# Expert layer: each kind of load on a queue of its own, in the order of the text, and a third weight tile asked for ahead

## The chip, the cores and the metric

The kernel runs on one core of one Trainium2 chip. The metric is device time in microseconds (us) of one execution, and a version is judged by the median of several runs. TensorE (PE in the profile) multiplies, VectorE (DVE) and ScalarE (ACT) do elementwise work, GpSimd (POOL) does a little elementwise work and the gathers, and SyncE (SP) only issues loads and stores. SP, ACT and POOL can each issue DMAs; each of them takes its instructions in order, so an instruction that waits holds up all that stand behind it on its engine.

## The reference, cut to what matters

The program is two transformer blocks, one behind the other. The change lies in the expert layer ("peer") of the first: 16384 single-neuron experts, of which each token picks 128 (8 heads with 16 each).

```python
def peer(xn, wq, keys, u, v):
    ...
    v1, i1 = lax.top_k(s1, PEER_TOPK)
    v2, i2 = lax.top_k(s2, PEER_TOPK)
    cand = (v1[..., :, None] + v2[..., None, :]).reshape(...)
    sc, ci = lax.top_k(cand, PEER_TOPK)
    e = i1[ci // PEER_TOPK] * PEER_NKEYS + i2[ci % PEER_TOPK]
    g = jax.nn.softmax(sc, axis=-1)
    hid = jnp.einsum('thkd,td->thk', u[e], xb)
    a = jax.nn.gelu(hid, approximate=False) * g
    return jnp.einsum('thk,thkd->td', a, v[e])
```

## The kernel before, in words

For 384 of the 512 tokens the kernel does not gather. It computes the hidden value of every expert and every token, sets the weights of the experts that were not picked to zero, and multiplies everything with all of v. The experts are cut into 128 blocks of 128 ("an expert" below is such a block, and a pair is two of them, even and odd). For the other 128 tokens it gathers the picked rows of u and v (`Rows`) and works on them with DVE.

The layer has three stretches.

- **Building** (`hidden`, 61 pairs). For each pair, two tiles of u (512 KB each, `raw`) come in on SP. ACT makes the high part `whi` of a tile, DVE the low part `wlo`, PE does 48 matmuls, ACT applies gelu, and the result goes to DRAM (`Gd`). Beside it runs a side stream, paced by estimated costs (`T16`, `T256`, `TLK`, `BUILD`, `ROW`, summed into `SHARE` and `UPACE`): first four blocks of top-k on DVE (`topk_block`), then 96 builds (`build`) of the choice weights (DVE `hot`, ACT `hot` and `ab`, PE `aps`), which go to DRAM in pieces (`Ad`), and all along the gathers of u and their dot products (`row`, `rhid`).
- **Changeover**. The last 16 pieces of `Ad` are stored, the last three pairs of `hidden` are done, and the first choice weights are read back.
- **Multiplying** (loop over `order`, 124 experts, then the last 4 together). Each expert takes a tile of v (`raw`, 512 KB), its hidden values (`gt`, one load of 384 KB for a pair, three buffers) and its choice weights (`at`, one load of 768 KB for four experts, two buffers). DVE multiplies them in place (`gt<-gt,at`, called G below), ACT and DVE split the product into `ah` and `al`, and PE does 24 matmuls. One row step (`ro`) on DVE goes with each expert, with a gather of v on POOL four steps ahead.

The order of instructions on each engine is set by a scheduler that starts from the order of the text and moves work by its own estimates, unless `keep_in_program_order` pins it. Before, all loads of `raw`, `gt` and `at` in the multiplying stretch stood on SP, in an order that the scheduler had made. `raw` has two buffers, `whi` and `wlo` three, `ah` and `al` five, a gathered row four.

Of the kernel before, what the change touches and what calls it, by code (L numbers as in the profile page):

```python
# [22 lines left out]
NM = 16  # L23
# [55 lines left out]
def setup(tc, es, A):  # L79
    g = Ctx()  # L80
    nc = tc.nc
    g.tc, g.nc, g.A = tc, nc, A
    g.const = es.enter_context(tc.tile_pool(name="const", bufs=1))
    g.res = es.enter_context(tc.tile_pool(name="res", bufs=1))
    g.wp = es.enter_context(tc.tile_pool(name="wp", bufs=3))
    g.np_ = es.enter_context(tc.tile_pool(name="np", bufs=2))
    c = g.const

    def cin(name, shape, now=True):
        t = c.tile(shape, F32, name="c_" + name)  # L90
        if now:
            nc.sync.dma_start(t, A[name])
        return t

    g.cin = cin
    g.vec = cin("vecs", [P, NVEC])
    g.ident = cin("ident", [P, P], False)
    g.ones = c.tile([P, P], F32, name="ones")
    nc.gpsimd.memset(g.ones, 1.0)
    g.eps = c.tile([P, 1], F32, name="eps")  # L100
    nc.gpsimd.memset(g.eps, EPS)
    g.zero = c.tile([P, 1], F32, name="zero")
    nc.gpsimd.memset(g.zero, 0.0)
    g.pre = {}
    g.queue = []
    g.h = [None] * KT
    h_tiles(g)
    return g


def h_tiles(g):
    for k in range(KT):
        g.h[k] = g.res.tile([P, T], F32, tag=f"h{k}", name=f"h{k}")
# [7 lines left out]
def wsrc(g, name, idx):  # L121
    a = g.A[name]
    for i in idx:
        a = a[i]
    return a


def wload(g, src, pool, hl):

    nc = g.nc  # L130
    _, a, b = src.shape
    raw = g.wp.tile([P, a, b], F32, tag="raw", name="raw", bufs=2)
    nc.sync.dma_start(raw, src)
    hi = pool.tile([P, a, b], F32R, tag="whi", name="whi", bufs=hl)
    nc.scalar.activation(hi, raw, AF.Copy)  # L135
    lo = pool.tile([P, a, b], F32R, tag="wlo", name="wlo", bufs=hl)
    nc.vector.tensor_tensor(lo, raw, r32(hi), op=ALU.subtract)  # L137
    return hi, lo


def wpre(g, name, *idx):

    key = (name, idx)
    if key not in g.pre:
        g.pre[key] = wload(g, wsrc(g, name, idx), g.wp, 3)


def wget(g, name, *idx):

    key = (name, *idx)  # L150
    wpre(g, *key)
    if key in g.queue[:1]:
        g.queue.pop(0)
        for k in g.queue[:2]:
            wpre(g, *k)
    return g.pre.pop((name, idx))


# [755 lines left out]

NK = 128
TOPK = 16
LAST = 4
N1 = 122
PARTS = 4
# [10 lines left out]

UH = 120

T16, T256, TLK, BUILD, ROW = 1.65, 2.3, 1.6, 1.5, 1.36
TOPKS = 16 * T16 + 3 + 8 * T256 + 8 * TLK + 2
BUILDS = NCK * (0.8 + CH // 4 * BUILD)
UPACE = UH * ROW / (3 * TOPKS + BUILDS)
# [3 lines left out]
class Rows:  # L940
# [29 lines left out]
    def choose(self, lists):  # L970
# [4 lines left out]
        else:  # L975
            t = self.p.tile([P, 3, NJ], F32, name="rl")
            n = 8 // RG
            nc.scalar.activation(t[0:GT].rearrange("p i (a b) -> p i a b", b=TOPK), lists[0:GT, :, 0:n], AF.Copy)
            for r in range(1, RG):
                nc.scalar.dma_start(t[r * GT:(r + 1) * GT].rearrange("p i (a b) -> p i a b", b=TOPK), lists[0:GT, :, r * n:(r + 1) * n])  # L980
            l = [t[:, i] for i in range(3)]
# [54 lines left out]
def peer_block(g, ni, tail):  # L1036

    tc, nc, A = g.tc, g.nc, g.A
    with ExitStack() as es:
        dr = es.enter_context(tc.tile_pool(name="p_dram", bufs=1, space=DRAM))  # L1040
        Gd = [dr.tile([P, 2, ND], F32, name=f"Gd{i}") for i in range(NK // 2)]
        Ad = dr.tile([NCK, P, NK, CH], F32, name="Ad")
        Hd = [dr.tile([P, S], F32, name=f"Hd{k}") for k in range(KT)]

        gp = es.enter_context(tc.tile_pool(name="p_g", bufs=2))

        order = list(range(NK - LAST, NK)) + list(range(NK - LAST))
        acc = Acc(g, es, "p_mm", 5).of(S)
        rg = Rows(g, es)

        with ExitStack() as e1:
# [15 lines left out]
            for c2 in range(4):  # L1067
# [4 lines left out]
                for e in range(2):  # L1072
                    t = kp.tile([P, 512], F32, name=f"q{2 * c2 + e}")
# [15 lines left out]
            def topk_block(b):  # L1089

                v = tp.tile([P, 16, TOPK], F32, tag="v", name="v")
                ix = tp.tile([P, 16, TOPK], U32, tag="ix", name="ix")
                for i in range(4):
# [133 lines left out]
            out = []  # L1227

            def weights():

                for b in range(4):
                    for n, c in enumerate(topk_block(b)):
                        yield c
                        if n == 12 and GT < b * P:
                            chosen[b - 1] = tokens_last(b - 1)
                for _ in range(8):
                    yield 1.0
                chosen[3] = tokens_last(3)
                e2.close()
                ab = e1.enter_context(tc.tile_pool(name="p_ab", bufs=2))  # L1240
                for c in range(NCK):
                    yield from build(ab, c)
                while out:
                    nc.scalar.dma_start(*out.pop(0))
                    yield 0.5

            def side():
                owed = 0.0
# [10 lines left out]

        lp = es.enter_context(tc.tile_pool(name="p_l", bufs=LAST + 1))  # L1260
        pp = psum_pool(g, es, "p_acc", 1)

        def four_in(i):

            at = lp.tile([P, NCK, 4, CH], F32, tag="at", name="at", bufs=2)
            (nc.sync if i < NK - LAST else nc.gpsimd).dma_start(at, Ad[:, :, i:i + 4].rearrange("c p e t -> p c e t"))
            return at

        def two_in(i):

            gt = lp.tile([P, 2, ND], F32, tag="gt", name="gt", bufs=3)
            if i < NK - LAST:
                nc.sync.dma_start(gt, Gd[i // 2])
            return gt


        ats, gts = {}, {}

        def expert(n):
            i = order[n]  # L1280
            for m in range(n - n % 4, min(n + 5, NK), 4):
                if order[m] not in ats:
                    ats[order[m]] = four_in(order[m])
            for m in range(n - n % 2, min(n + 4, NK), 2):
                if order[m] not in gts:
                    gts[order[m]] = two_in(order[m])
            return weighted(ats[i - i % 4][:, :, i % 4], gts[i - i % 2][:, i % 2])
# [6 lines left out]
            split(g, gt, ah, al)  # L1294
            return ah, al

        ats[NK - LAST] = four_in(NK - LAST)
        for i in range(NK - LAST, NK, 2):
            gts[i] = two_in(i)

        for i in range(N1 // 2, NK // 2):
# [7 lines left out]
        for n, i in enumerate(order[:-LAST]):  # L1309
            a = expert(n)  # L1310
            vh, vl = wget(g, "peer_v", i)
            mmx(nc, a, [(accs[k][:, GT:], (vh[:, k], vl[:, k])) for k in range(KT)], False, False)
            rg.steps()
            if 8 <= n < 8 + KT:
                nc.sync.dma_start(g.h[n - 8][:, NM:], Hd[n - 8])

        last = [(expert(n), wload(g, wsrc(g, "peer_v", (order[n],)), lp, LAST)) for n in range(NK - LAST, NK)]
        for k in range(KT):
            for j, (a, (vh, vl)) in enumerate(last):
                mm3(nc, accs[k][:, GT:], (vh[:, k], vl[:, k]), a, False, False)  # L1320
# [26 lines left out]
class GdnNorm:  # L1347
# [8 lines left out]
    def load(self, es):  # L1356

        g = self.g
        self.sp = es.enter_context(g.tc.tile_pool(name="gn_sp", bufs=3))
        for k in range(KT):  # L1360
            g.nc.gpsimd.dma_start(g.h[k][:, 0:NM], g.A["metaT"][k])

    def step(self, k):
        g, nc = self.g, self.g.nc
# [860 lines left out]
```

## Time and profile before

| | |
|---|---|
| median of 3 runs | 3694.72 us (3683.52 to 4518.06) |
| the profiled execution | 3688.95 us, its span 3686.8 us |
| busy share of the span | PE 95%, DVE 64%, ACT 43%, POOL 22% |
| granted TensorE clock, mean | 0.973 of full speed |
| DMA | 557.58 MB, 151 GB/s over the span |

The busy shares are means over stretches with different limits, so the table says little about one stretch. PE's busy time runs from the first to the last end of pipelined matmuls; its idle time and what ended it are more telling. 2.15 us lie between the span and the time of the profiled execution.

### The profile page before, as it was taken

The page shows a single profiled execution, that of the slowest core. Times are in us where ns is not written, and L with a number is a line of the kernel's source. Part 1 is how long each engine was busy: PE and PEld are TensorE (multiplying, and loading weights), DVE is VectorE, ACT ScalarE, POOL GpSimd, SP SyncE. Part 2 cuts the span into 40 slices and gives each one's busy share as a digit, 9 for nine tenths or more (in the row PEclk, how much of TensorE's full clock was granted, in tenths as well). Part 3 has the DMA queues.
Part 4 walks back from the last instruction along what each step waited for, and adds up shares of the span by engine and source line. Part 5 has one row for each costly group of instructions (what it writes and reads, how often), then busy time and mean ns, then how long its engine had stood idle before and what let it go on. Part 6 is the DMA issues. An engine that isn't in the chain of part 4 may idle for free. (4 is left out here: it accounts for less than half of the span.)

```text
span 3686.8 us, 56387 instructions
## 1 busy us (share of the span) xinstructions
PE 3492.9 (95%) x21979; PEld 3189.4 (87%) x21979; DVE 2375.6 (64%) x4299; ACT 1580.8 (43%) x2998; POOL 810.4 (22%) x781
## 2 busy tenths in 40 slices
PE   8999999888899978989999999999999999999999
PEld 6777888888899978988988899999899998877887
DVE  5764457899977757766777667766653345565333
ACT  4555333333498833333336445444432235443222
POOL 2431010443422222332323223222110002110000
PEclk9999999999999989999999899999999999999999
DMA  4223233677777888888872211111122222212232
GB/s 132 80 81 91 86 124 123 237 251 248 243 269 266 294 306 302 315 305 304 309 275 72 64 55 57 51 56 51 49 85 92 91 88 87 73 60 95 92 97 92
DMA packets 188370, 557.58 MB, mean 151 GB/s; under 512 B 19617, under 2 KB 43938, under 8 KB 188104
## 3 DMA queue, kind: packets, MB, share of 16 engines
q1 hardware_dynamic: 123460, 362.26, 29.9%
q0 software_dynamic: 41408, 142.07, 11.4%
q10 hardware_dynamic: 23236, 49.65, 3.5%
q8 instruction: 173, 2.83, 0.3%
q14 instruction: 93, 0.76, 0.1%
HBM read 492.20 MB, written 55.41 MB: 149 GB/s over the span
## 5 line engine op out<-in xcount | busy, mean ns | idle before, releaser
L135 ACT ACTIVATE whi<-raw 128x1024 fp32r<-128x1024 f32 x562 | 595.6, 1060 | 1428.6 <-PE ps L76 706.5
L72 PE MATMUL ps<-xh,wlo 128*128 128x264 f32 (+2 forms) x3296 | 1056.0, 333 | 57.6 <-DVE wlo L137 57.4
L71 PE MATMUL ps<-xh,whi 128*128 128x264 f32 (+2 forms) x3296 | 1071.9, 337 | 36.5 <-ACT whi L135 19.7
L137 DVE TENSOR_TENSOR wlo<-raw,whi 128x1024 fp32r<-128x1024 f32 x562 | 711.2, 1266 | 381.5 <-ACT whi L135 378.2
L76 PE MATMUL ps<-xl,whi 128*128 128x264 f32 (+2 forms) x3296 | 815.1, 332 | 7.5 <-DVE xl L267 7.4
L72 PEld LDWEIGHTS ps<-xh,wlo 128*128 128x128 f32 x3296 | 631.6, 192 | 98.6 <-DVE wlo L137 68.6
L71 PEld LDWEIGHTS ps<-xh,whi 128*128 128x128 f32 x3296 | 632.5, 192 | 74.4 <-ACT whi L135 24.7
L76 PEld LDWEIGHTS ps<-xl,whi 128*128 128x128 f32 x3296 | 565.3, 193 | 39.8 <-DVE xl L267 9.3
L994 POOL DMA_INDIRECT row<-in_peer_v_dram,rix x128 | 177.0, 1383 | 428.7 <-DVE ro L1007 389.2
L994 POOL DMA_INDIRECT row<-in_peer_ur_dram,rix x128 | 172.2, 1346 | 378.5 <-DVE row L1003 277.9
L71 PE MATMUL ps<-ah,whi 128*128 128x264 f32 (+1 forms) x768 | 230.2, 320 | 0.0
L72 PE MATMUL ps<-ah,wlo 128*128 128x264 f32 (+1 forms) x768 | 229.9, 320 | 0.0
L55 PE MATMUL ps<-ah,whi 128*128 128x384 f32 x640 | 220.9, 345 | 0.0
L56 PE MATMUL ps<-ah,wlo 128*128 128x384 f32 x640 | 220.0, 344 | 0.0
L56 PE MATMUL acc<-ah,wlo 128*128 128x384 f32 x384 | 136.3, 355 | 48.7 <-DVE wlo L137 48.6
L258 POOL TENSOR_TENSOR ssum<-ssum,sq 128x512 f32<-128x512 f32 (+1 forms) x49 | 75.2, 1541 | 460.5 <-ACT sq L257 460.0
L1003 DVE SCALAR_TENSOR_TENSOR row<-row,rx 128x1024 f32<-128x1024 f32 x128 | 170.2, 1330 | 7.8 <-DMA row<-in_peer_ur_dram,rix 7.8
L1291 DVE TENSOR_TENSOR gt<-gt,at 128x384 f32<-128x384 f32 x128 | 66.4, 555 | 157.3 <-DMA gt<-Gd 141.9
L76 PE MATMUL ps<-al,whi 128*128 128x264 f32 (+1 forms) x768 | 163.3, 321 | 0.0
L1007 DVE SCALAR_TENSOR_TENSOR ro<-row,rhid,ro 128x1024 f32<-128x1024 f32 x127 | 162.3, 1278 | 0.1
L1179 DVE TENSOR_TENSOR hot<-iota,lt 128x1024 f32<-128x1024 f32 x96 | 117.2, 1223 | 68.0 <-PE aps L1198 67.8
L71 PEld LDWEIGHTS ps<-ah,whi 128*128 128x128 f32 x768 | 144.3, 188 | 11.4
(427 smaller groups left out, 6199.7 us busy)
## 6 DMA issues: line engine op xcount, KB each, us to landing
raw<-in_peer_u_dram SPq DMA_DIRECT2D x128, 512.0 KB, 5.6
raw<-in_peer_v_dram SPq DMA_DIRECT2D x128, 512.0 KB, 5.0
raw<-in_ff_up_dram SPq DMA_DIRECT2D x64, 512.0 KB, 3.4
raw<-in_ff_down_dram SPq DMA_DIRECT2D x64, 512.0 KB, 3.4
Ad<-ab ACTq DMA_DIRECT2D x96, 256.0 KB, 5.1
raw<-in_gdn_in_dram SPq DMA_DIRECT2D x48, 512.0 KB, 3.4
Gd<-G ACTq DMA_DIRECT2D x62, 384.0 KB, 5.5
at<-Ad SPq DMA_DIRECT2D x31, 768.0 KB, 6.6
```

The source lines that it names most:

```text
L55: nc.tensor.matmul(out, lh, rh, start=start, stop=False)
L56: nc.tensor.matmul(out, ll, rh, start=False, stop=False)
L71: nc.tensor.matmul(segs[s][0], lh, xh[:, sl], start=start, stop=False)
L72: nc.tensor.matmul(segs[s][0], ll, xh[:, sl], start=False, stop=False)
L76: nc.tensor.matmul(segs[s][0], lh, xl[:, sl], start=False, stop=stop)
L135: nc.scalar.activation(hi, raw, AF.Copy)
L137: nc.vector.tensor_tensor(lo, raw, r32(hi), op=ALU.subtract)
L258: g.nc.gpsimd.tensor_tensor(self.t[:, 0:n], self.t[:, 0:n], sq[:, 0:n], op=ALU.add)
L994: nc.gpsimd.indirect_dma_start(out=t, out_offset=None, in_=(self.U, self.V)[e], in_offset=bass.IndirectOffsetOnAxis(ap=self.ix[:, j:j + 1] ...
L1003: o = nc.vector.scalar_tensor_tensor(t, t, 1.0, self.x, op0=ALU.mult, op1=ALU.mult, accum_out=a)
L1007: o = nc.vector.scalar_tensor_tensor(self.o, t, a, self.o, op0=ALU.mult, op1=ALU.add)
L1179: nc.vector.tensor_tensor(o, iota.unsqueeze(1).unsqueeze(1).to_broadcast([P, 2, 4, NK]), lt[:, 0:2, 4 * t4:4 * t4 + 4].unsqueeze(3).to_bro ...
```

## The change

Six things are changed. (1) In the multiplying stretch the loads of `gt` go to ACT's queue, those of `at` to POOL's, and SP keeps the weights and eight loads of `h`. (2) All these loads, the eight `h` loads and the `metaT` loads are pinned to the order of the text. (3) The last 16 stores of `Ad` go from ACT to POOL, with no pacing between them. (4) The load of a third weight tile is asked for ahead (`wstart`); `raw` still has two buffers. (5) The estimates of the side stream's costs are altered. (6) `LAST` is split into `FIRST` and `LAST`, both 4 as before.

```diff
-def wload(g, src, pool, hl):
+def wraw(g, src):
     nc = g.nc
     _, a, b = src.shape
     raw = g.wp.tile([P, a, b], F32, tag="raw", name="raw", bufs=2)
     nc.sync.dma_start(raw, src)
+    return raw
+
+def wload(g, raw, pool, hl):
...
+def wstart(g, name, *idx):
+    key = (name, idx)
+    if key not in g.raw and key not in g.pre:
+        g.raw[key] = wraw(g, wsrc(g, name, idx))
...
     if key not in g.pre:
-        g.pre[key] = wload(g, wsrc(g, name, idx), g.wp, 3)
+        wstart(g, name, *idx)
+        g.pre[key] = wload(g, g.raw.pop(key), g.wp, 3)
...
         for k in g.queue[:2]:
             wpre(g, *k)
+        for k in g.queue[2:3]:
+            wstart(g, *k)
...
-T16, T256, TLK, BUILD, ROW = 1.65, 2.3, 1.6, 1.5, 1.36
+T16, T256, TLK, BUILD, ROW = 1.8, 2.55, 1.6, 1.3, 1.4
...
                 while out:
-                    nc.scalar.dma_start(*out.pop(0))
-                    yield 0.5
+                    tc.keep_in_program_order(nc.gpsimd.dma_start(*out.pop(0)))
...
-            (nc.sync if i < NK - LAST else nc.gpsimd).dma_start(at, Ad[:, :, i:i + 4].rearrange("c p e t -> p c e t"))
+            tc.keep_in_program_order(nc.gpsimd.dma_start(at, Ad[:, :, i:i + 4].rearrange("c p e t -> p c e t")))
...
-            if i < NK - LAST:
-                nc.sync.dma_start(gt, Gd[i // 2])
+            if i < NK - FIRST:
+                tc.keep_in_program_order(nc.scalar.dma_start(gt, Gd[i // 2]))
...
             if 8 <= n < 8 + KT:
-                nc.sync.dma_start(g.h[n - 8][:, NM:], Hd[n - 8])
+                tc.keep_in_program_order(nc.sync.dma_start(g.h[n - 8][:, NM:], Hd[n - 8]))
...
-            g.nc.gpsimd.dma_start(g.h[k][:, 0:NM], g.A["metaT"][k])
+            g.tc.keep_in_program_order(g.nc.gpsimd.dma_start(g.h[k][:, 0:NM], g.A["metaT"][k]))
```

How the instructions move is seen best at three places. The line numbers of the changed kernel are 17 or 18 higher than those of the kernel before.

**The changeover.** On ACT before, behind the last build (`Ad` are the stores of choice weights, `Gd` of hidden values):

```order
L1199 ACTIVATE ab<-aps 128x4x128
L1201 DMA Ad<-ab 128x512
L1244 DMA Ad<-ab 128x512 x16
L135 ACTIVATE whi<-raw 128x1024 x2
L1221 ACTIVATE G<-ps 128x384 x2
L1223 DMA Gd_4666<-G 128x768
L135 ACTIVATE whi<-raw 128x1024 x2
```

On POOL now, behind the last gathers of u:

```order
L1262 DMA Ad<-ab 128x512 x16
L1283 DMA at<-Ad 128x6x256
L1378 DMA h_11799<-in_metaT_dram 128x16
L1378 DMA h_11800<-in_metaT_dram 128x16
L1378 DMA h_11801<-in_metaT_dram 128x16
L1378 DMA h_11802<-in_metaT_dram 128x16
L1378 DMA h_11803<-in_metaT_dram 128x16
L1378 DMA h_11804<-in_metaT_dram 128x16
L1378 DMA h_11805<-in_metaT_dram 128x16
L1378 DMA h_11806<-in_metaT_dram 128x16
L1283 DMA at<-Ad 128x6x256
L1012 DMA row<-in_peer_v_dram,rix 128x1024 x3
```

The 16 stores no longer stand ahead of `whi` on ACT, and the first load of `at`, which needs all stores, no longer stands ahead of the weights on SP.

**The middle of the multiplying stretch, DVE and ACT.** The numbers tell tiles apart; `gt` has three buffers, so `gt_13396` before takes the buffer of `gt_13160`, three pairs back. DVE before:

```order
1556 L1291 TENSOR_TENSOR gt_13318<-gt_13318,at_13278 128x384 x2
1557 L267 TENSOR_TENSOR al_13282<-gt_13160,ah_13281 128x384
1558 L137 TENSOR_TENSOR wlo_13131<-raw_13127,whi_13129 128x1024
1559 L1007 SCALAR_TENSOR_TENSOR ro_4688<-row_13039,rhid_4689,ro_4688 128x1024
1560 L267 TENSOR_TENSOR al_13322<-gt_13160,ah_13321 128x384
1561 L137 TENSOR_TENSOR wlo_13171<-raw_13167,whi_13169 128x1024
1562 L1007 SCALAR_TENSOR_TENSOR ro_4688<-row_13077,rhid_4689,ro_4688 128x1024
1563 L1291 TENSOR_TENSOR gt_13396<-gt_13396,at_13278 128x384 x2
```

DVE now, where the pair behind these rows, `gt_13472`, takes the buffer of `gt_13234`, the pair ahead of them:

```order
1561 L1308 TENSOR_TENSOR gt_13314<-gt_13314,at_13274 128x384 x2
1562 L144 TENSOR_TENSOR wlo_13323<-raw_13285,whi_13321 128x1024
1563 L1025 SCALAR_TENSOR_TENSOR ro_4688<-row_13231,rhid_4689,ro_4688 128x1024
1564 L284 TENSOR_TENSOR al_13436<-gt_13314,ah_13435 128x384
1565 L284 TENSOR_TENSOR al_13476<-gt_13314,ah_13475 128x384
1566 L144 TENSOR_TENSOR wlo_13361<-raw_13325,whi_13359 128x1024
1567 L1025 SCALAR_TENSOR_TENSOR ro_4688<-row_13271,rhid_4689,ro_4688 128x1024
1568 L1308 TENSOR_TENSOR gt_13392<-gt_13392,at_13274 128x384 x2
1569 L144 TENSOR_TENSOR wlo_13401<-raw_13363,whi_13399 128x1024
1570 L1025 SCALAR_TENSOR_TENSOR ro_4688<-row_13311,rhid_4689,ro_4688 128x1024
```

ACT now:

```order
1157 L142 ACTIVATE whi_13281<-raw_13245 128x1024
1158 L1290 DMA gt_13314<-Gd18_4623 128x768
1159 L142 ACTIVATE whi_13321<-raw_13285 128x1024
1160 L283 ACTIVATE ah_13435<-gt_13314 128x384
1161 L283 ACTIVATE ah_13475<-gt_13314 128x384
1162 L142 ACTIVATE whi_13359<-raw_13325 128x1024
1163 L1290 DMA gt_13392<-Gd19_4624 128x768
1164 L142 ACTIVATE whi_13399<-raw_13363 128x1024
```

G of a pair stood three pairs ahead of the pair's `al`, and so used the last buffer; now `al` follows G of the same pair. The load of `gt` now stands one `whi` ahead of the two `ah` that need it.

**The middle of the multiplying stretch, POOL.** Before there were only gathers here. Now:

```order
356 L1012 DMA row_13271<-in_peer_v_dram,rix_4691 128x1024
357 L1283 DMA at_13274<-Ad_4669 128x6x256
358 L1012 DMA row_13311<-in_peer_v_dram,rix_4691 128x1024
359 L1012 DMA row_13351<-in_peer_v_dram,rix_4691 128x1024
360 L1012 DMA row_13389<-in_peer_v_dram,rix_4691 128x1024
361 L1012 DMA row_13429<-in_peer_v_dram,rix_4691 128x1024
362 L1283 DMA at_13432<-Ad_4669 128x6x256
```

Each load of `at` stands behind a gather that waits for the row step four back (`ro`) on DVE.

In the building stretch the order on ACT shows the first `ab` of the builds behind the 84th weight tile of u instead of the 79th, and on DVE the last top-k of 256 candidates behind the 76th instead of the 70th.

## Rows read from the trace of the kernel before

**Rows 1.** Windows: bounds, length; busy PE PEld DVE ACT POOL; clock, DMA share, GB/s

```profile
600.00:1298.30 698.30, 636.64 (x3826) 619.58 (x3824) 599.67 (x1294) 401.26 (x757) 243.17 (x153) 0.98 0.74 251
1298.30:1346.00 47.70, 27.67 (x125) 25.55 (x126) 15.97 (x22) 11.69 (x18) 4.60 (x6) 0.75 0.84 305
1346.00:1400.00 54.00, 51.87 (x296) 50.91 (x295) 39.20 (x51) 17.38 (x24) 14.22 (x12) 1.00 0.90 310
1400.00:1900.00 500.00, 456.48 (x2513) 445.81 (x2512) 352.28 (x424) 155.40 (x210) 153.22 (x109) 0.97 0.86 306
```

**Rows 2.** Waits, 1400 to 1900: total us, times, longest

```profile
PE acc L56 <- DVE wlo L137: 43.4, 29, 3.3
...
DVE gt L1291 <- DMA gt<-Gd: 129.8, 50, 5.2
...
SPq L1273 <- DVE al L267: 76.1, 51, 6.2
```

**Rows 3.** Timeline of PE: first matmul of two experts in a row

```profile
1608.43 0.34 PE L55 MATMUL acc<-ah,whi 128*128 128x384 f32 x1
...
1612.59 0.34 PE L55 MATMUL acc<-ah,whi 128*128 128x384 f32 x1
```

**Rows 4.** The tile raw, 1400 to 1900: ns min/median/max, first and last start

```profile
L135 ACT ACTIVATE whi<-raw x105: 1056/1061/1067, 1402.3 to 1896.2; 128x1024 fp32r<-128x1024 f32 x105
```

**Rows 5.** Timeline of DVE, then ACT and SP, around one pair

```profile
1605.38 0.56 DVE L267 TENSOR_TENSOR al<-gt,ah 128x384 fp32r<-128x384 f32 x1
1605.85 1.22 DVE L137 TENSOR_TENSOR wlo<-raw,whi 128x1024 fp32r<-128x1024 f32 x1
1606.99 1.28 DVE L1007 SCALAR_TENSOR_TENSOR ro<-row,rhid,ro 128x1024 f32<-128x1024 f32 x1
1611.07 1.03 DVE L1291 TENSOR_TENSOR gt<-gt,at 128x384 f32<-128x384 f32 x2 [2.80 <-DMA gt<-Gd]
...
1614.82 0.55 DVE L267 TENSOR_TENSOR al<-gt,ah 128x384 fp32r<-128x384 f32 x1
...
1614.69 0.51 ACT L266 ACTIVATE ah<-gt 128x384 fp32r<-128x384 f32 x1
...
1615.39 0.33 SPq L1273 DMA_DIRECT2D gt<-Gd  x1
```

**Rows 6.** DMA issues, 1400 to 1900: count, KB each, median us to landing

```profile
raw<-in_peer_v_dram SPq DMA_DIRECT2D x104, 512.0 KB, 5.1
gt<-Gd SPq DMA_DIRECT2D x52, 384.0 KB, 5.2
at<-Ad SPq DMA_DIRECT2D x25, 768.0 KB, 6.6
```

**Rows 7.** Timeline of the changeover: ACT, SP and PE

```profile
1298.33 16.43 ACTq L1244 DMA_DIRECT2D Ad<-ab  x16
...
1328.66 1.06 ACT L135 ACTIVATE whi<-raw 128x1024 fp32r<-128x1024 f32 x1 [11.09 <-DMA raw<-in_peer_u_dram]
...
1319.73 0.38 SPq L1266 DMA_DIRECT2D at<-Ad  x1
...
1342.24 0.42 PE L55 MATMUL acc<-ah,whi 128*128 128x384 f32 x1
```

**Rows 8.** Timeline of POOL: the one load of at, and two gathers

```profile
1320.25 0.88 POOL L1266 DMA_DIRECT2D at<-Ad  x1 [15.01 <-DMA Gd<-G]
...
1605.74 2.15 POOL L994 DMA_INDIRECT row<-in_peer_v_dram,rix  x1 [3.99 <-DVE ro L1007]
1608.54 0.94 POOL L994 DMA_INDIRECT row<-in_peer_v_dram,rix  x1 [0.66 <-DVE ro L1007]
```

**Rows 9.** The tile at, 1319 to 1321: landing of the load that POOL issued

```profile
DMA to landing us min/median/max: 8.6/8.6/8.6
```

**Rows 10.** Windows of the building stretch, with top-k and with the builds

```profile
640.00:1000.00 360.00, 313.36 (x1736) 301.41 (x1735) 341.79 (x883) 122.53 (x177) 158.96 (x95) 0.96 0.73 245
1005.00:1298.00 293.00, 279.55 (x1837) 275.75 (x1835) 217.26 (x238) 258.52 (x547) 78.69 (x56) 1.00 0.81 273
```

More of the change, by code (lines that the diff above doesn't have):

```diff
@@ L104, in setup @@
     g.pre = {}
+    g.raw = {}
     g.queue = []
@@ L133, in wload @@
     nc.sync.dma_start(raw, src)
+    return raw
+def wload(g, raw, pool, hl):
+    nc = g.nc
+    _, a, b = raw.shape
     hi = pool.tile([P, a, b], F32R, tag="whi", name="whi", bufs=hl)
@@ L916 @@
 TOPK = 16
+FIRST = 4
 LAST = 4
@@ L1045, in peer_block @@
         gp = es.enter_context(tc.tile_pool(name="p_g", bufs=2))
-        order = list(range(NK - LAST, NK)) + list(range(NK - LAST))
+        order = list(range(NK - FIRST, NK)) + list(range(NK - FIRST))
         acc = Acc(g, es, "p_mm", 5).of(S)
@@ L1295, in weighted @@
             return ah, al
-        ats[NK - LAST] = four_in(NK - LAST)
-        for i in range(NK - LAST, NK, 2):
+        ats[NK - FIRST] = four_in(NK - FIRST)
+        for i in range(NK - FIRST, NK, 2):
             gts[i] = two_in(i)
@@ L1314, in peer_block @@
             if 8 <= n < 8 + KT:
-                nc.sync.dma_start(g.h[n - 8][:, NM:], Hd[n - 8])
-        last = [(expert(n), wload(g, wsrc(g, "peer_v", (order[n],)), lp, LAST)) for n in range(NK - LAST, NK)]
+                tc.keep_in_program_order(nc.sync.dma_start(g.h[n - 8][:, NM:], Hd[n - 8]))
+        last = [(expert(n), wload(g, wraw(g, wsrc(g, "peer_v", (order[n],))), lp, LAST)) for n in range(NK - LAST, NK)]
         for k in range(KT):
```

## The prediction

> **What bounds the kernel now.** I read the windows by stretch first, to see where time can be won [rows 1]. The order of instructions is altered only in the expert layer, between about 600 and 1950 us, so the rest of the 3686.8 us stays as it is. In the layer PE is idle for 61.7 us of the building stretch (698.3 less 636.6), for 20 us of the changeover of 47.7 us, where its granted clock is 0.75 as well, and for 43.5 us of the 500 us between 1400 and 1900.
>
> Then I read the waits [rows 2]. In the multiplying stretch PE waits 43.4 us for `wlo`. DVE, which makes it, waits 129.8 us for loads of `gt`, in 50 of 52 pairs. SP waits 76.1 us for `al` before it can issue those loads. So the question is why `gt` is late.
>
> An expert that PE does without a wait takes 1612.59 - 1608.43 = 4.16 us [rows 3], 24 matmuls of 0.173 us. In fact an expert takes (1896.2 - 1402.3)/104 = 4.75 us [rows 4]. The timeline of one pair shows a ring of waits that gives just this [rows 5]. G starts at 1611.07 when its load has landed; behind it DVE does `al`, `wlo`, `ro` and the second `al`, which ends at 1615.37; SP issues the next `gt` at 1615.39, because only this `al` frees a buffer. That is 4.32 us. The load then takes 5.2 us [rows 6], and DVE stands before the next G after only `wlo` and `ro`, some 2.4 us. Ring: 4.32 + 5.2 = 9.5 us for a pair, 4.76 for an expert, against the measured 4.75. Not the amount of data and not PE sets this pace, but one load that is asked for too late.
>
> The changeover has another cause [rows 7]. ACT issues 16 stores of `Ad` from 1298.33 on for 16.43 us, with `whi` behind them; SP holds the weights of the next pair behind a load of `at` that waits for those stores until 1319.73, and ACT's `whi` idles another 11.09 us for them. From the last build to the first matmul of the multiplying stretch 1342.24 - 1298.33 = 43.9 us pass, in which PE has only three pairs of 48 matmuls to do, 3 x 48 x 0.173 = 25 us.
>
> **The change, part by part.** The sum is made against the profiled execution, 3688.95 us, which is 0.16% under the median of 3694.72.
>
> *Changeover.* With the stores on POOL, `whi` and the weights flow on, and PE can do its three pairs in 25 us. What is late next is `at`. POOL issues 16 stores; taken at the 0.88 us of its one load of `at` [rows 8] that is 14 us, the last takes some 5 us to land (1314.76 to 1319.73 before [rows 7]), the load of `at` 0.88 and 8.6 us [rows 9], G and `ah` 1.0: about 29 us, against 25 for PE. So 43.9 becomes 26 to 39 us, the upper end if a store on POOL costs half way from 0.88 to a gather's 2.15 us, 16 x 1.5 = 24; I take 29. **Gain 15 us** (5 to 18).
>
> *Building.* The new estimates stretch the top-k over 2.5 more pairs (five weight tiles). With top-k DVE is the bound, 341.8 busy of 360 us; with the builds it is PE, 279.6 of 293, ACT next with 258.5 [rows 10]. Into the first part go 5 x 1.22 of `wlo` and 3 row steps of 1.28, 10 us more on DVE, while the 20.8 us more for PE fit into its 46.6 us of idle time there. The second part loses 2.5 x 8.3 = 20.8 us of PE; its ACT floor falls by some 8 to 250, so PE goes on setting it. **Gain 10 us** (from a loss of 5, if ACT and PE get into each other's way with builds packed 15% closer, to a gain of 20).
>
> *The third weight tile.* `raw` keeps two buffers, and SP has the weights in the same order as before, so a third load is asked for no sooner than a buffer is free. Nothing, either way, in the building stretch and in the feed-forward layers, where SP's order is unaltered.
>
> *Eight loads of `h`*, 256 KB each, go from the building stretch into the first experts. At 306 GB/s they are 0.86 us each, 7 us of transfer at a place where the engines of the DMA are 0.90 busy [rows 1]. **Loss 2 us** (0 to 7).
>
> *Multiplying.* On ACT the load of `gt` stands behind one `whi`, and its buffer was freed long before, so the ring through `al` is gone. Four limits are next.
> - PE itself: 4.16 us.
> - The new ring of `gt` on ACT: load 5.2 [rows 6], both G 1.03, the second `ah` 0.51, then the next `whi` starts and with it the next issue: 6.8 us for a pair, 3.4 for an expert. Only a landing after 8.6 us, as of the one load of `at` [rows 9], would make it 5.1.
> - The weights. In a pair, the odd `wlo` stands behind both G. From `gt`'s issue to its end are 5.2 + 1.03 + 1.22 = 7.4 us, then a buffer is free and the next weights take 5.1: 12.5 us over three experts, 4.2 each. It grows with the latency of the loads: with 6.0 us for both it is 14.25, and the pace is back at 4.75.
> - The ring of `at` on POOL: a row step ends, its gather is issued (0.94 to 2.15 [rows 8]), then `at` (0.88 to the same 2.15), which lands after 6.6 to 8.6; then from G to the row step that releases the next one DVE has 3.75 us to the second `al` [rows 5] and `al`, `wlo`, `ro` behind it, 6.6 in all. Low 15.0, high 19.5, middle 17.2 us over four experts: 4.3 each.
>
> And the DMA must carry it. An expert moves 306 x 4.75 = 1.45 MB, and occupies the DMA engines for 0.86 x 4.75 = 4.09 us [rows 1]. At 4.35 us an expert they would be 0.94 busy, more than any stretch held [rows 1], at 4.16 us 0.98. I take **4.35 us**, a little above the middle of both rings, since latency grows with load. About 110 experts run at the present pace (until 1400 the pace is 54/(296/24) = 4.4): 110 x 0.40 = **gain 44 us** (0 to 62).
>
> Sum: 15 + 10 - 2 + 44 = 67 us. 3689 - 67 = **3622 us**, 1.8% faster, which is less than the 2% that a measurement of this kernel can about tell from no change.
>
> A rule of the Trainium skill speaks for the opposite of the POOL queue (page "SBUF — State Buffer", sections "SBUF: two separate sides" and "Who interferes with whom"). It says that GpSimd must write the descriptors of a DMA that it issues, that certain DVE instructions lock it out meanwhile, and that ACT or SP should issue such a load. The trace agrees in kind: a gather took 2.15 us with DVE busy and 0.94 with DVE idle [rows 8]. What this would do to `at` is the second rival.
>
> **The rivals.**
>
> *A: the DMA is full.* None of these stretches held more than 0.90 [rows 1]. If that is the ceiling, an expert takes 4.09/0.90 = 4.54 us and the gain there is 110 x 0.21 = 23: 3689 - 15 - 10 + 2 - 23 = 3643 us. For it: the loads of all three kinds take 5 to 7 us by now [rows 6], and a fuller DMA makes that longer. Against it: the waits above are for buffers, not for data on its way.
>
> *B: `at` through POOL is the new bound, and the kernel gets slower.* A load of `at` is 128 x 6 pieces of 1 KB, a gathered row 128. If POOL's time goes by pieces, an issue under load costs six times 0.94 to 2.15, middle 9.3 us, and the ring becomes 1.5 + 9.3 + 6.6 + 6.6 = 24 us over four experts, 6.0 each: 110 x 1.25 = 138 us more, 3689 + 138 - 23 = 3804 us. It decides from 19.8 us on (4.96 an expert), an issue of about 5 us. Against it: the one load of `at` on POOL took 0.88 us [rows 8], though DVE was idle then.
>
> *C: separate queues bring no pace.* The pace stays at 4.75, because some other load takes over the role of `gt` (weights at 6 us, above), and only the changeover and the building gain: 3689 - 25 + 2 = 3666 us. The Trainium skill has a rule to this effect (page "DMA: Bandwidth & Descriptors", section "Issuing engines are not separate DMA queues"): all issuers share the same 16 engines, and several of them save no more than issue time. Here the time saved is that in which SP stood and waited with other loads behind it, 76.1 us for `al` alone [rows 2], so I do not expect this.
>
> **How the numbers follow.** Forecast, 3585 to 3640: 0.60. A, 3630 to 3660: 0.20. C, 3655 to 3690: 0.11. B, over 3700: 0.09. The range: the best ends give 18 + 20 + 62 = 100 us, 3589; on the other side it takes in C with a loss in building, 3689 + 2 less a few. So **3586 to 3690**. Faster by over 2% means below 3621, a little over half of the forecast's 0.60 and what lies below: 0.40. Slower by over 2% is most of B: 0.08. Within 2%: 0.52.
>
> **What would show it.** Right: in the multiplying stretch DVE no longer waits for `gt` in every pair, or does so without PE waiting for `wlo`; `whi` in a steady row every 4.2 to 4.5 us; DMA share above 0.90; no block of 16 stores on ACT, and the first matmul of that stretch within 30 us of the last build. Wrong: DVE waiting for `at` at every fourth expert, or POOL spending 5 us on one issue (B); loads that land after 6 us and more at a share of 0.90 (A); `whi` waiting for weights in every expert with a pace of 4.7 (C); PE idle among the builds, with ACT full (the building term). It would be wrong altogether if PE stalls appeared behind a late `ah`, for which I have found no ring.

## The result, and the profile after

The changed kernel takes **3718.7 us** (median of 4 runs, 3715.3 to 3723.0) against 3692.0 us for the kernel before on the same chips: a ratio of **1.0081, 95% interval 1.0058 to 1.0104**. The ratio leaves out one execution of the kernel before that took 4518 us. It is 0.8% slower, where 1.8% faster was forecast, and its time lies outside the range. The profiled execution took 3718.55 us, its span is 3716.8 us.

The windows of the kernel after, at its own borders (bounds, length; busy PE PEld DVE ACT POOL; clock, DMA share, GB/s):

```profile
640.00:1000.00 360.00, 323.02 (x1759) 309.42 (x1758) 341.60 (x874) 121.89 (x174) 156.90 (x95) 0.96 0.73 249
1005.00:1314.80 309.80, 285.19 (x1826) 279.48 (x1825) 219.87 (x241) 261.51 (x558) 74.97 (x51) 0.98 0.76 255
1314.80:1343.80 29.00, 21.87 (x103) 19.57 (x103) 8.45 (x9) 8.88 (x15) 14.41 (x26) 0.84 0.93 334
1346.00:1400.00 54.00, 53.90 (x306) 53.58 (x305) 38.50 (x54) 17.52 (x24) 14.57 (x14) 0.98 0.87 298
1400.00:1900.00 500.00, 447.76 (x2462) 438.14 (x2461) 349.57 (x419) 155.85 (x205) 154.30 (x135) 0.97 0.87 308
```

The rows answer to [rows 1, 10]. The last build ends at 1314.8 instead of 1298.3, the changeover takes 29.0 instead of 43.9 us, and between 1400 and 1900 PE is idle for 52.2 us instead of 43.5. So the account of the span is, stretch by stretch:

| stretch | before | after | change | forecast |
|---|---|---|---|---|
| to the last build | 1298.3 | 1314.8 | +16.5 | -10 |
| last build to first matmul of multiplying | 43.9 | 29.0 | -14.9 | -15 |
| multiplying, to its last matmul | 609.3 | 622.9 | +13.6 | -42 |
| from there to the first matmul on `oh` | 207.5 | 217.9 | +10.4 | 0 |
| the rest | 1527.8 | 1532.2 | +4.4 | 0 |
| span | 3686.8 | 3716.8 | +30.0 | -67 |

The forecast of multiplying holds the 2 us for the loads of `h`. The two lines above the sum hold the same instructions in both kernels; how much of them belongs to one execution is taken up with experiment 12. There multiplying took 631.1 us with the same kernel, so single profiles don't tell differences of some 8 us in that stretch from no difference.

Waits of the kernel after, 1400 to 1900 (total us, times, longest):

```profile
PE acc L56 <- DVE wlo L144: 50.5, 25, 5.1
...
DVE gt L1308 <- DMA gt<-Gd: 98.2, 27, 7.0
DVE gt L1308 <- DMA at<-Ad: 38.4, 6, 7.6
...
ACT whi L142 <- DMA raw<-in_peer_v_dram: 246.4, 82, 7.8
```

The row of `whi` in the same stretch:

```profile
L142 ACT ACTIVATE whi<-raw x103: 1039/1061/1068, 1401.1 to 1896.4; 128x1024 fp32r<-128x1024 f32 x103
```

SP no longer waits for `al`, and DVE waits for `gt` in 27 pairs instead of 50 [rows 2]: that ring is gone. But each of the waits is longer (3.6 instead of 2.6 us on average), `at` has joined, and an expert takes (1896.4 - 1401.1)/102 = 4.86 us instead of 4.75 [rows 4]. The timeline of POOL, ACT and DVE shows the ring that took its place:

```profile
1596.49 0.90 POOL L1283 DMA_DIRECT2D at<-Ad  x1
...
1599.07 0.33 ACTq L1290 DMA_DIRECT2D gt<-Gd  x1
...
1608.30 1.03 DVE L1308 TENSOR_TENSOR gt<-gt,at 128x384 f32<-128x384 f32 x2 [5.73 <-DMA gt<-Gd]
1609.24 1.22 DVE L144 TENSOR_TENSOR wlo<-raw,whi 128x1024 fp32r<-128x1024 f32 x1
...
1615.40 1.06 ACT L142 ACTIVATE whi<-raw 128x1024 fp32r<-128x1024 f32 x1 [4.57 <-DMA raw<-in_peer_v_dram]
1616.37 0.92 ACT L283 ACTIVATE ah<-gt 128x384 fp32r<-128x384 f32 x2
1618.66 1.06 ACT L142 ACTIVATE whi<-raw 128x1024 fp32r<-128x1024 f32 x1 [1.37 <-DMA raw<-in_peer_v_dram]
1618.68 0.33 ACTq L1290 DMA_DIRECT2D gt<-Gd  x1
```

A `gt` load is issued at 1599.07 and DVE has it at 1608.30, 9.2 us later. Only behind both G comes `wlo`, which ends at 1610.46 and frees a buffer for weights; these reach ACT at 1615.40, 4.9 us later. ACT then does this `whi`, both `ah` and waits for the next weights; only behind the next `whi` does it issue the `gt` load of two pairs on, at 1618.68. One turn is 19.6 us and carries two pairs (the `gt` load of the pair between goes out inside it): 4.90 us an expert.

The long step is the landing of `gt`, and it is long only beside a load of `at`. Of the `gt` loads between 1400 and 1900, 26 were issued within 5 us of an `at` load and 25 were not. DVE waited for 20 of the first kind, 93.0 us in all, and had them 8.6 us behind their issue (median). It waited for 7 of the second kind, 5.2 us in all, and had them behind 5.1 us. The profile of experiment 12 repeats this: 8.9 us (21 loads) against 5.9 (5). Before, with both kinds on SP, it was 5.2 against 4.4 us. Since `at` comes once for two pairs, about every second `gt` load meets one.

The changeover in the timeline, ACT, POOL and PE:

```profile
1313.81 1.02 ACT L1217 ACTIVATE ab<-aps 128x512 f32<-128x512 f32 x1 [0.35 <-PE aps L1216]
...
1324.23 1.06 ACT L142 ACTIVATE whi<-raw 128x1024 fp32r<-128x1024 f32 x1 [6.84 <-DMA raw<-in_peer_u_dram]
...
1315.39 4.87 POOL L1262 DMA_DIRECT2D Ad<-ab  x9 [2.94 <-issue]
...
1327.49 2.42 POOL L1262 DMA_DIRECT2D Ad<-ab  x4 [1.46 <-DMA Ad<-ab]
1337.10 0.87 POOL L1283 DMA_DIRECT2D at<-Ad  x1 [7.19 <-DMA raw<-in_peer_v_dram]
...
1343.84 0.69 PE L55 MATMUL acc<-ah,whi 128*128 128x384 f32 x1 [3.84 <-DMA h<-in_metaT_dram]
```

The chain is the one of the prediction, stores, then `at`, then the first matmul, though its links differ. A store on POOL costs 0.54 us, not 0.88, but waits for earlier stores stand between them, so that the sixteen end 15.1 us behind the last build. The load of `at` goes out 7.2 us behind the last store, not 5 (a wait that the trace puts down to a load of weights). From there to the first matmul 6.7 us pass, where 10.5 were summed.

### The profile page after: what moved, and what is told of

Its sections match the earlier page's. It is cut to its first block, busy times and chain, and to the rows that moved or that the text cites. A ratio compares the mean times of both kernels' runs of the same rounds, so it can differ in the third digit from the quotient of the medians.

```text
span 3716.8 us, 56286 instructions
## 1 busy us (share of the span) xinstructions
PE 3521.9 (95%) x21979; PEld 3214.1 (86%) x21979; DVE 2383.1 (64%) x4299; ACT 1584.7 (43%) x2998; POOL 819.8 (22%) x828
## 5 line engine op out<-in xcount | busy, mean ns | idle before, releaser
L1012 POOL DMA_INDIRECT row<-in_peer_v_dram,rix x128 | 151.6, 1185 | 406.0 <-DVE ro L1025 374.0
```

The source lines that it names most:

```text
L1012: nc.gpsimd.indirect_dma_start(out=t, out_offset=None, in_=(self.U, self.V)[e], in_offset=bass.IndirectOffsetOnAxis(ap=self.ix[:, j:j + 1] ...
```

## The experiments

All times are medians with the ratio to the kernel before run beside them; "multiplying" is the time from its first to its last matmul in the profile, 128 experts. "Old estimates" are the five numbers of the kernel before.

**1. Only the estimates back.**

```diff
-T16, T256, TLK, BUILD, ROW = 1.8, 2.55, 1.6, 1.3, 1.4
+T16, T256, TLK, BUILD, ROW = 1.65, 2.3, 1.6, 1.5, 1.36
```

> The changed kernel with the five estimates of the side stream set back, everything else as changed. In the changed kernel the last build ended 16.5 us later than before (1314.8 against 1298.3). Theory: the estimates did that, by packing the builds closer (23.5 instead of 20.5 for ten weight tiles); then the last build ends near 1298 again and the time is about 3702 us (3698 to 3706). Rival: it came from the order of the loads (the third weight tile, the pins); then the last build stays near 1314 and the time near 3718 us.

Measured 3701.5 us, ratio 1.0041 (1.0020 to 1.0061). The last build in the timeline of ACT:

```profile
1294.79 1.02 ACT L1217 ACTIVATE ab<-aps 128x512 f32<-128x512 f32 x1 [0.35 <-PE aps L1216]
```

It ends 19 us sooner than in the changed kernel. The estimates cost 17 us by the medians, 15 by the ratios, and the rival falls. Multiplying took 636.3 us against 609.3, so the loss that is left lies there.

**2. The stores on POOL alone**, in the kernel before.

```diff
-                    nc.scalar.dma_start(*out.pop(0))
-                    yield 0.5
+                    tc.keep_in_program_order(nc.gpsimd.dma_start(*out.pop(0)))
```

> The kernel before with one part alone: the last 16 stores of choice weights on POOL, without pacing. Theory: the changeover shrinks from 43.9 to about 29 us, as in the changed kernel, and nothing gives it back: 3692 - 15 = 3677 us. Rival: SP still holds the first load of choice weights ahead of the weights of the next pair, so PE stands as long as before and the time stays near 3690 us.

Measured 3685.5 us, ratio 1.0003 (0.9987 to 1.0019): no gain that can be measured. In the profile the changeover fell from 43.9 to 33.0 us (29 were expected), and multiplying grew from 609.3 to 618.5. The scheduler gave that stretch another order as well (`al` and G alternate singly in more places on DVE). So whether the gain was given back by this order, by the ring or by one execution alone, isn't shown.

**3. `gt` asked for a pair earlier**, and **4. a real third buffer for the weights of v**, both on the changed kernel.

```diff
-            for m in range(n - n % 2, min(n + 4, NK), 2):
+            for m in range(n - n % 2, min(n + 6, NK), 2):
```

> The changed kernel with the load of gt asked for one pair earlier in the text (n + 6 instead of n + 4). Theory ring: the pace of 4.86 us an expert comes from the time between the issue of a gt load and its landing (7.6 us where DVE waited for it, 4.6 before) and the weights behind it; with a pair more ahead DVE stops waiting for gt and the pace falls to 4.3 to 4.5 us, 120 x 0.4 = 48 us less: about 3670 us. Theory DMA full: the pace is bytes by what the DMA carries at a share of 0.86 to 0.90, the waits go over to weights or choice weights, the pace stays at 4.75 to 4.86 and the time at 3710 to 3720 us.

```diff
-    raw = g.wp.tile([P, a, b], F32, tag="raw", name="raw", bufs=2)
+    g.nv += v
+    raw = g.vp.tile([P, a, b], F32, tag="rawx", name="raw", bufs=1) if v and g.nv % 3 == 0 else g.wp.tile([P, a, b], F32, tag="raw", name="raw", bufs=2)
```

> The changed kernel with a real third buffer for the weights of v (room is made by two instead of three scratch buffers behind the layer). Theory ring: the weights ring of 3 experts becomes one of 4, (7.6 + 1.0 + 1.2 + 5.7)/4 = 3.9 us an expert, so PE or the load of gt sets the pace, 4.3 to 4.5 us: 3670 us or so. Theory DMA full: pace 4.75 to 4.86, loads of weights that are longer on their way by what they are asked for earlier, 3710 to 3720 us.

The third run took 3756.8 us (1.0183, 1.0151 to 1.0216), the fourth 3698.2 us (1.0045, 1.0027 to 1.0064). Neither theory had the third, and the fourth fell between its two. In both, DVE stopped waiting for `gt` (2 waits and 1) and waited for `at` instead, 24 and 25 times in 500 us, at every fourth expert. The timeline of POOL and DVE in the fourth shows why:

```profile
1606.79 0.90 POOL L1285 DMA_DIRECT2D at<-Ad  x1
...
1626.50 0.90 POOL L1285 DMA_DIRECT2D at<-Ad  x1
...
1616.99 1.03 DVE L1310 TENSOR_TENSOR gt<-gt,at 128x384 f32<-128x384 f32 x2 [4.95 <-DMA at<-Ad]
...
1623.88 2.62 POOL L1014 DMA_INDIRECT row<-in_peer_v_dram,rix  x1 [2.26 <-DVE ro L1027]
```

The load lands 10.2 us after its issue. Its successor stands behind a gather that waits for a row step, and goes out 9.5 us after G has started: 19.7 us for four experts, 4.93 each. So behind the ring of the weights stands a second one of almost the same length, and taking the first away leaves the other. (In the changed kernel itself DVE waited for `at` only 6 times.) The third run lost 38 us more than the changed kernel; there the scheduler also tore the pairs of G on DVE apart, 51 single ones instead of 5, and whether that or the ring of `at` made the loss stays open.

**5. Gathers of 512 bytes** instead of 4 KB in the multiplying stretch.

```diff
+                o_, i_ = t[:, 0:W], self.V.rearrange("a (n b) -> (a n) b", b=W)
```

> The changed kernel, but each gathered row of v from the fifth on brings 512 bytes instead of 4 KB (other numbers; the same count of gathers, pieces and row steps). An expert then moves about 0.98 instead of 1.44 MB. Theory: loads land late because several of them share the DMA engines, and the rings of waits turn at the speed of their landing; then gt lands about 5 us behind its issue instead of 7.6, the pace falls from 4.86 to 4.2 or 4.3 us, and the time to about 3645 us. Rival: loads land late for a reason of the queues themselves (the issue behind a waiting instruction); then landing and pace stay, 4.7 to 4.9 us, 3705 to 3720 us.

Measured 3644.1 us (one run). The window, 1400 to 1850:

```profile
1400.00:1850.00 450.00, 436.99 (x2472) 430.36 (x2471) 348.95 (x417) 152.02 (x204) 171.50 (x135) 0.99 0.70 229
```

From the issue of a `gt` load to the G that waited for it passed 7.3 us (median of 11 such pairs) instead of 7.7 (of 27), for `at` 7.9 (of 18) instead of 10.5 (of 6), and multiplying took 567.0 us, 4.43 an expert. With fewer bytes `at` lands sooner, `gt` is late in fewer pairs, and the rings turn faster; the time came as the theory says, while its landing of 5 us for `gt` did not.

**6. Old estimates, third buffer, `at` on SP.** The cut shows the last of the three edits; the others are those of 1 and 4.

```diff
-            tc.keep_in_program_order(nc.gpsimd.dma_start(at, Ad[:, :, i:i + 4].rearrange("c p e t -> p c e t")))
+            tc.keep_in_program_order(nc.sync.dma_start(at, Ad[:, :, i:i + 4].rearrange("c p e t -> p c e t")))
```

> The changed kernel with the old estimates, a third buffer for the weights of v, and the loads of choice weights on SP instead of POOL (still pinned). In the run with the third buffer DVE waited 142 us for choice weights, 25 times in 500 us, each asked for some 10 us too late by a gather on POOL. Theory ring: with them asked for at the weights' pace these waits go and the pace falls from 4.61 to about 4.35 us; with the changeover of 30 us the time is about 3645 us. Theory DMA full: nothing goes under 4.55 us an expert (share 0.90), and the time is about 3670 us. Third: the loads on SP stand in each other's way again, pace 4.75, 3690 us.

Measured **3608.2 us, ratio 0.9807 (0.9780 to 0.9834)**: it beats both kernels, and the best of its theories by 37 us. (The 4.61 us that the expectation gives for run 4 is 4.82 by its multiplying time.) Its window:

```profile
1400.00:1850.00 450.00, 448.02 (x2582) 446.95 (x2580) 369.46 (x443) 167.01 (x219) 198.94 (x113) 1.00 0.96 354
```

What is left of PE's wait for `wlo` between 1400 and 1900:

```profile
PE acc L56 <- DVE wlo L146: 0.3, 1, 0.3
```

PE is busy for 448.0 of 450 us, and multiplying takes 543.6 us, 4.25 an expert, close to the 4.16 of PE alone [rows 3]. The DMA engines carry 354 GB/s at a share of 0.96: theory "DMA full" falls, for this kernel and for the one before.

**7. The third buffer in the kernel before.** The edit is that of experiment 4.

> The kernel before with a third buffer for the weights of v alone (and two instead of three scratch buffers behind the layer). My reading of the kernel before says that the ring through al, gt's buffer and the landing of gt sets its pace; then another buffer for the weights changes nothing, pace 4.75, 3685 to 3692 us. If the ring of the weights bounds it as well, the pace falls to 4.5 or so and the time to 3660 us.

Measured 3676.6 us, 0.9982 (0.9965 to 0.9999); multiplying 593.5 us, 4.64 an expert. DVE waited for `gt` 50 times, 128.4 us, as before. So the weights are not what bounds the kernel before, which speaks for the ring through `al`; the buffer is worth 0.2% there, a little more than the nothing that was expected.

**8 to 11. Which queue.** Old estimates throughout, the loads pinned as changed; the edits replace `nc.scalar` for `gt` or `nc.gpsimd` for `at` by `nc.sync`, and 11 has the third buffer. Wherever `gt` goes back to SP (8, 10, 11) the scheduler also gives DVE another order, G, G, `al`, `wlo`, `ro`, `al` instead of G, G, `wlo`, `ro`, `al`, `al`, and ACT one with the two `ah` apart; runs that differ in the queue of `at` alone keep the order of DVE.

> The changed kernel with the old estimates and the loads of gt and of choice weights on SP, still pinned to the order of the text: the queues taken back, the order kept. With three queues and old estimates it took 3701 us. Theory: three queues put more loads on their way at once and each lands later, which costs the 0.1 to 0.2 us an expert; then the pace is 4.75 or less and the time 3680 to 3690 us. Rival: the order of the text costs it, with the load of gt only one weight tile ahead of its use; then the pace stays at 4.85 to 5.0 and the time at 3700 us or above.

> The changed kernel with the old estimates and the loads of choice weights on SP, but with the two buffers for the weights: the version of 3608 us without its third buffer. Theory: the ring through the load of gt, G, wlo and the weights behind it (three experts a turn) bounds the changed kernel, and it is still there; pace 4.8 to 5.0, 3690 to 3702 us. Rival: the choice weights on POOL bounded it, the third buffer only helped beside; pace 4.5 or less, 3660 us or less.

> The changed kernel with the old estimates and the loads of gt back on SP, those of choice weights left on POOL. All three apart took 3701 us, all on SP 3685. If the queue of gt on ACT, where its load stands behind whi and whi behind weights, costs the 16 us, this one takes 3685 us. If the choice weights on POOL cost them, it stays at 3700 us.

> The version of 3608 us with the loads of gt on SP as well: one queue for all three kinds, order of the text, three buffers for the weights. Theory: the buffer and the time of asking count, not the queue; pace 4.16 to 4.3 and 3608 to 3625 us. Rival: on one queue a load of weights that waits for its buffer holds up the load of gt behind it, as before; pace 4.5 to 4.7, 3655 to 3680 us.

**13 to 15. `at` on POOL or ACT**, for the questions that these left open.

> The version of 3608 us with the loads of choice weights back on POOL: old estimates, third buffer, three queues. Theory place: on POOL a load of choice weights stands behind a gather that waits for a row step of DVE, so it is asked for about 10 us ahead of its use and lands after 10; then DVE waits for it at every fourth expert as with the new estimates, pace 4.6 to 4.7, 3675 to 3690 us. Rival: the new estimates or the position of the experts caused those waits; then pace 4.2 to 4.4 and under 3640 us.

> The version of 3608 us with the loads of choice weights on ACT, where each stands ahead of the ah of the pair before. Theory place: it is asked for some 6 us sooner than on POOL, which is enough; no waits for choice weights, pace 4.16 to 4.3, 3608 to 3630 us. Rival: only SP, where they stand among the weights, serves them in time; then pace 4.4 to 4.7 and 3645 to 3690 us.

> The changed kernel with the old estimates, two buffers for the weights, and the loads of choice weights on ACT. On POOL they gave 3701 us, on SP 3678, with DVE waiting for them only three times in 500 us on POOL. If their place behind the gathers on POOL costs the 23 us, this one takes 3675 to 3685 us. If it is any third load that doesn't stand among the weights, it takes 3695 to 3705 us.

All with the old estimates:

| weights | `gt` on | `at` on | run | median us | ratio (95%) | multiplying us |
|---|---|---|---|---|---|---|
| 2 buffers | SP | SP | 8 | 3684.7 | 0.9993 (0.9973 to 1.0014) | 613.4 |
| 2 | SP | POOL | 10 | 3680.1 | 0.9978 (0.9959 to 0.9998) | 611.4 |
| 2 | ACT | SP | 9 | 3677.6 | 0.9974 (0.9958 to 0.9991) | 600.8 |
| 2 | ACT | ACT | 15 | 3697.5 | 1.0022 (0.9999 to 1.0044) | 628.1 |
| 2 | ACT | POOL | 1 | 3701.5 | 1.0041 (1.0020 to 1.0061) | 636.3 |
| 3 buffers | SP | SP | 11 | 3694.5 | 1.0011 (0.9995 to 1.0026) | 626.3 |
| 3 | ACT | POOL | 13 | 3685.5 | 1.0003 (0.9988 to 1.0019) | 620.7 |
| 3 | ACT | ACT | 14 | 3632.0 | 0.9853 (0.9827 to 0.9879) | 553.6 |
| 3 | ACT | SP | 6 | 3608.2 | 0.9807 (0.9780 to 0.9834) | 543.6 |

With two buffers the queues matter little, 24 us from best to worst: three queues cost 17 us against one, and either of the two loads back on SP gives them back (8 to 10). With three buffers the queues decide over 86 us, that of `at` alone over 77 (6, 13, 14). Waits of DVE between 1400 and 1900 with everything on SP (run 11), and between 1400 and 1850 with `at` on POOL (run 13):

```profile
DVE gt L1310 <- DMA gt<-Gd: 123.9, 47, 7.5
```

```profile
DVE gt L1310 <- DMA at<-Ad: 134.8, 23, 7.6
```

On SP the load of `gt` stands behind weights that wait for their buffer, and comes late in 47 pairs. The timeline of SP in run 11 shows it:

```profile
1609.66 0.43 SPq L1292 DMA_DIRECT2D gt<-Gd  x1
1612.08 7.31 SPq L135 DMA_DIRECT2D raw<-in_peer_v_dram  x2
1619.45 0.42 SPq L1292 DMA_DIRECT2D gt<-Gd  x1
```

The next `gt` goes out 9.8 us behind the one before it, once the second weight load ahead of it has got a buffer: 4.9 us an expert, and 626.3/128 is 4.89. The expectation that the queue doesn't count (11) was wrong; how much of the 86 us comes from the changed orders on DVE and ACT isn't shown. (A count of late `gt` proves nothing by itself: run 6 waits for `gt` in 34 pairs, 79.3 us, and PE stands still for none of it.)

On POOL `at` comes late at nearly every fourth expert (its issues in run 13 are at 1601.44 and 1620.54, 19.1 us a turn), which confirms "place" in 13 and 14: on ACT not one wait for `at` is left, though run 14 came 2 us above its range. Experiment 9 came out between its two expectations: 24 us less than experiment 1, but 69 more than with the third buffer.

In 15, ACT served no better than POOL, against "place": with two buffers and `gt` on ACT it costs some 20 us that `at` isn't on SP, be it on POOL or on ACT; with `gt` on SP it costs nothing (10 against 8). DVE waited for `at` three times on POOL and never on ACT, so it isn't lateness of `at`. The traces point to lateness of `gt` beside `at`: of DVE's waits for `gt`, 112.2 of 112.5 us in run 1 and 88.8 of 114.4 in run 15, but 38.5 of 100.5 in run 9, fall on loads issued within 5 us of an `at` load. That this makes the 20 us, no run shows.

**12. The changed kernel again.**

> The changed kernel, unaltered. In its profile the stretch behind the expert layer, whose instructions are those of before, took 217.8 us instead of 207.5, at a lower clock (0.80 to 0.91 instead of 0.86 to 0.99). Theory: that is luck of one execution; then it is between 204 and 215 us here, and the median is near 3710 us. Rival: it belongs to the program; then 216 to 219 us again and 3718 us.

Measured 3718.4 us, 1.0075 (1.0043 to 1.0108). The stretch behind the layer took 213.8 us, in the range of the first expectation, while the median is that of the second. Over all profiles here it took from 201.1 to 224.6, and the version with 224.6 (run 9) had one of the better medians. The line below it in the account was 1528.8 us here, against 1532.2 and, before, 1527.8. So part of the 10.4 and most of the 4.4 us belong to one execution; how much stays open. The loss as a whole belongs to the kernel.

## Why the prediction was wrong, step by step

Forecast and measured span differ by 97 us: 56 of them in multiplying, 26 in building, 15 in the stretches behind, which were put at nothing and belong in part to one execution.

**The building term failed, in its sign.** It forecast a gain of 10 us and at worst a loss of 5; the last build came 16.5 us later, and taking back the estimates undid it (experiment 1). The windows of the two kernels up to the first build and from there to the last, before and after:

```profile
600.00:997.20 397.20, 351.84 (x1957) 338.83 (x1955) 375.41 (x1049) 134.76 (x194) 162.76 (x96) 0.96 0.69 233
997.20:1298.30 301.10, 284.81 (x1869) 280.75 (x1869) 224.26 (x245) 266.50 (x564) 80.41 (x58) 1.00 0.81 274
```

```profile
600.00:1016.70 416.70, 376.28 (x2051) 361.37 (x2051) 390.65 (x1058) 141.61 (x205) 167.81 (x101) 0.96 0.70 238
1016.70:1314.80 298.10, 273.49 (x1769) 267.81 (x1767) 212.09 (x228) 258.12 (x553) 70.49 (x47) 0.98 0.76 253
```

The first part was priced at 10 us more and took 19.5: DVE did 15.2 us more work in it and stood idle for 4.3 more. It did six weight tiles more and five row steps, where five and three were summed, and a row step of this part takes 1.4 us, not the 1.28 that were read in the multiplying stretch. The second was priced at 20.8 us less, on the ground that PE would go on setting its end; it became only 3.0 us shorter. PE lost 100 instructions and 11.3 us of busy time there, but its idle time rose from 16.3 to 24.6 us and its granted clock fell from 1.00 to 0.98. ACT's busy time fell from 266.5 to 258.1, so ACT isn't the bound either. What grew are the waits of DVE for PE and of PE for DVE (total us, times, longest; the second part, before and after):

```profile
DVE hot L1179 <- PE aps L1198: 67.8, 49, 3.2
...
PE ps L72 <- DVE wlo L137: 12.1, 16, 1.2
```

```profile
DVE hot L1197 <- PE aps L1216: 78.0, 55, 3.3
...
PE ps L72 <- DVE wlo L144: 20.3, 16, 2.2
```

PE waits 8.2 us more for `wlo`, nearly all of the 8.3 us by which its idle time grew. So the failed step is the rule that the busiest engine's work sets the length of a part: builds packed closer wait for each other, and no engine's sum of work tells that.

**The changeover held**: 29.0 us against 29, and 31.6 in the second profile of the same kernel. That the sum met it to the tenth is luck: its links were off by 1 to 4 us both ways. Alone it was worth nothing measurable (experiment 2).

**The third weight tile**: at nothing, rightly, so far as `raw` kept two buffers; the change doesn't do what its words say. With a real third buffer it would have been the term that matters: 69 us between runs 9 and 6.

**The multiplying term failed, 44 us of gain against 13.6 of loss.** The mechanism was right in part: the ring through `al` is gone, and both rings that were named as next were found turning, that of the weights in the changed kernel, that of `at` in runs 4 and 13. Both were mis-sized, mainly by their landing times. The ring of the weights was summed to 12.5 us for three experts with a landing of 5.2 us [rows 6]; traced, `gt` took 9.2 us and the turn was 19.6 us for four, of which 3.3 us are work and a wait on ACT that the sum left out. The prediction said that 6.0 us would bring the pace back to 4.75, and took the short value. The 5.2 us were right for the `gt` loads that meet no load of `at` (5.1 us where DVE waited), and wrong for the half that do (8.6). That meeting was no term of the sum: a landing read on one queue was carried over to three, where `at` and `gt` are on their way together. The ring of `at` was bounded by 15.0 and 19.5 us and taken at 17.2; traced it is 19.1 to 19.7. Each ring was also given as a reason for 4.2 or 4.3 by itself, while removing one of them brought 24 us (9) or 16 (13) against experiment 1, and both together 93 (6).

**Rival C came nearest**: "some other load takes over the role of gt". It gave 4.75 us an expert, 4.87 were measured; its 3666 us missed by 53, since it kept the gain in building and left multiplying as it was. Its rule in the Trainium skill ("DMA: Bandwidth & Descriptors", "Issuing engines are not separate DMA queues") agrees for the change as made, 308 GB/s on three queues against 306 on one. It doesn't cover runs 6 and 13, which differ only in the queue of `at` and by 77 us: an engine that issues in order decides which load stands behind which wait. **Rival A falls**: the DMA carried a share of 0.96. **Rival B falls** by its mechanism, though the time came to lie where it put it, over 3700 us: an issue of `at` on POOL took 0.87 to 0.92 us, with DVE busy too. What the Trainium skill says of descriptors written by GpSimd ("SBUF — State Buffer", "SBUF: two separate sides") didn't show in it; whether DVE's instructions here are among those that it names, no run shows. Its place was right all the same: `at` on POOL bounds run 13, by the gather ahead of it. **The loads of `h`** weren't tried by themselves.

## What to carry to other kernels

Where a stretch is bound by a ring of waits, list every ring that is within some per cent of it before pricing its removal: here two of 19 to 20 us for four experts took the place of the one of 19.0, and only edits that broke both (a buffer, and a load asked for in time) brought PE to its own pace or near it. A landing time belongs to the queues and the neighbours under which it was read: where the change lets a load go out beside a bigger one, price the ring with the longest landing in the trace and not with the median. And an in-order queue is chosen by what stands ahead of a load on it, not by how many loads it has.

## What the runs showed of the hardware that was not expected

- The DMA engines held a share of 0.96 and 354 GB/s over 450 us (run 6), where it had looked like a ceiling at 0.90: all versions but 5, 6 and 14 show 0.83 to 0.90 there; `gt` landed there no later than at 308 GB/s (median 7.2 against 7.7 us where DVE waited).
- With PE idle for only 2 us of these 450 its granted clock was 1.00, the level of 2.4 GHz; with 30 to 60 us of scattered idle time in them it was 0.92 to 0.98 in the other versions with full gathers except run 14. In run 3, at 0.92 and with 60.0 us idle, PE was busy 390.04 us for 2044 matmuls, 0.191 each, against 448.02 for 2582, 0.174 each, in run 6: there idle time cost more than itself.
- A plain store of 256 KB costs POOL 0.54 us to issue (in the changeover) and a load of 768 KB 0.90, also while DVE works, where the gather ahead of it took 2.62 us (run 4).
